# A streaming-encoder block in float32: the operand's first transposes moved ahead of the gain vector's, and the weight groups of the first FFN begun after 16 standard steps in place of 12

## The chip, the cores and the metric

One core of one Trainium2 chip. The metric is the device time of one execution in microseconds; lower is better. Three timed runs of the kernel before are shown, and one execution was profiled.

## What is computed

One block over 256 frames of width 2048, in float32:

```python
x = x + 0.5 * swiglu_ffn(rmsnorm(x, g1), w_gate, w_up, w_down)      # D_FF = 5632
h = rmsnorm(x, gm)
proj = h @ w_in                                                     # 2048 x 11264
x = x + (sigmoid(gate_a) * attention(...) @ w_out_att
         + sigmoid(gate_r) * retention(...) @ w_out_ret) @ w_out
x = x + 0.5 * swiglu_ffn(rmsnorm(x, g2), w_gate2, w_up2, w_down2)
out = rmsnorm(x, gf)

def swiglu_ffn(x, w_gate, w_up, w_down):
    return (silu(x @ w_gate) * (x @ w_up)) @ w_down
```

The change touches the opening of the program and the first of the two FFNs.

## The kernel before

**Tiles.** The frames are two tiles of 128 (t = 0, 1). The transposed activations are the stationary operand of TensorE, the weights are streamed past it in tiles of 256 rows by 512 columns (0.5 MB). Float32 is kept by splitting both sides in a high and a low part: `split` (line 126, 127) casts a weight tile to its high part on ScalarE (`hi`) and subtracts on VectorE what is left (`lo`); `three` (lines 137, 138, 140) then makes three matmuls of 512 columns for each product: high by high, high by low, low by high. The split buffers are four (`SPLIT_BUFS`), the buffers of unsplit tiles five (`RAW_BUFS`).

**Steps.** The program is one list of steps, written in order. A *standard* step takes one weight tile for both frame tiles: 12 matmuls, one split. A *group* (class `Strassen`) makes the up and gate product of one block of 512 columns together, in 28 steps of 6 matmuls: three phases of eight steps (tiles `z12...`: group, phase, number, `r` or `s`) and a fourth of four. In the first phase VectorE also adds a pair of tiles for four of the steps (line 528), in the second it adds (line 583) and subtracts (line 570), and POOL then issues a transfer that accumulates into the tile (line 571). So a group step of the first two phases costs VectorE up to two operations of full size, where a standard step costs it one. The groups' unsplit tiles (`z12k`, `z12x`) are loaded by POOL (line 539), all others by SP (line 117).

**The order.** `weave` (line 670 on) first puts `lead` standard steps in the list. Then, behind each pair of a group's steps, it adds a standard step whenever its credit allows, unless the next standard job needs blocks that are not there yet (`needs`, `at_hand`). The standard jobs of the FFN are the gate and up products of blocks 9 and 10, eight steps each, and the down products in seven passes. The first is gate 9, then up 9, gate 10, and the down product of blocks 9 and 0:

```python
for _ in range(lead):
    next_standard()
rate = (len(queue) - apart) / (len(groups) * sum(SHARE))
```

The tiles of the first group are asked for eight steps ahead of it (`first = len(steps) - 8`), and POOL issues them behind a tiny operation that waits for the third block of the operand (`third_block`, line 804).

**The norm's work.** `Norm.put` (line 449) transposes two blocks of x on TensorE, scales them by the gain on ScalarE (line 462) and splits them (446, 447). It is called in the opening and in steps 1 to 6. The sums of blocks that the groups use as operands (`s5`, `s6`, `s3`, `s7`) are made by `add_up` on VectorE (lines 483 to 497, tiles `n1f`, `n1s5l` ...), up to step 18. The squares are summed on ScalarE in steps 8 to 11, and POOL raises the result to the power -0.5 (`n1rstd`, line 373). The gate of block 9 is passed through Silu in step 12; line 742 is the eviction of its up product (`f1g`), line 377 the low part of its transposes (`f1a9l`).

**The opening.** SP loads x and the first weight tiles; ACT's queue loads the identity and the gain vector. `turn` transposes the gain vector on TensorE (line 292) and copies it on VectorE (293). Then `prep_upto(1)` splits the first weight tile, here with casts on VectorE (line 161), and `n1.put(0, 0)` transposes the first two blocks.

Of the kernel before, what the change touches and what calls it, by code (L numbers as in the profile page):

```python
# [27 lines left out]
KC = 2  # L28
# [7 lines left out]
TAIL = 4  # L36
AHEAD = (2, 3)
HALF_K = D // P // 2
LEAD = 12
MIX_LEAD = 8  # L40
RET_WAIT = (14, 5)
HELD = 6
# [3 lines left out]
PASSES = ((9, 0), (1, 2), (10, 3), (4, 5), (6,), (7,), (8,))  # L46
# [26 lines left out]
def block_kernel(ctx: ExitStack, tc: tile.TileContext, x, g1, w1g, w1u, w1d, gm, w_in, rel, woa, wor, wo,  # L73
# [32 lines left out]
    def later(n, fn):  # L106
        due.setdefault(state["step"] + n, []).append(fn)
# [124 lines left out]
    def prep_upto(n):  # L232

        while state["prep"] < min(len(steps), n) and state["slots"]:
            s = steps[state["prep"]]
            load_some()
            state["slots"] -= 1
            s.prep()
            for ring in s.frees:
                room[ring] += 1  # L240
            state["prep"] += 1
        load_some()
# [142 lines left out]
    class Operand:  # L385
# [11 lines left out]
        def put(self, b, t, src):  # L397

            hi, lo = self.alloc(b)
            ts = slice(t * P, (t + 1) * P)  # L400
            ps = transpose4(src, f"{self.name}p{b}{t}").rearrange("p (i q) -> p i q", i=4)
            split_out(ps, hi[:, :, ts], lo[:, :, ts])
# [5 lines left out]
    class Norm:  # L408
# [37 lines left out]
            nc.scalar.copy(hi[:, js, :], src)  # L446
            nc.vector.tensor_sub(lo[:, js, :], src, hi[:, js, :].bitcast(F32))

        def put(self, b, half):
            if half == 0:  # L450
                self.raw[b] = act_tile(F32, f"{self.name}x{b}")
            raw = self.raw[b]
            ps = side_tile(f"{self.name}p{b}{half}")
            for i in range(2):
                k = 4 * b + 2 * half + i
                for t in range(NT):
                    nc.tensor.transpose(
                        ps[:, (2 * i + t) * P : (2 * i + t + 1) * P], xs[t][:, k * P : (k + 1) * P], id_sb
                    )
            for i in range(2):  # L460
                k = 4 * b + 2 * half + i
                nc.scalar.activation(
                    raw[:, 2 * half + i, :], ps[:, i * SEQ : (i + 1) * SEQ], AF.Copy, scale=self.gain[:, k : k + 1]
                )
            j = 4 * (b // 2) + 2 * half
            for t in range(NT):
                src = raw[:, 2 * half : 2 * half + 2, t * P : (t + 1) * P]
                self.split_to(f"a{t}{b % 2}", slice(j, j + 2), src)
            if half == 1 and not self.sums:
                del self.raw[b]  # L470
            elif half == 1 and b % 2 == 1:
                for i, key in enumerate(self.SUMS):
                    later(1 + 3 * i, lambda key=key: self.add_up(b // 2, key))
# [238 lines left out]
    def ffn(name, norm, wg, wu, wd, after, start=None):  # L712


        nblocks = DFF // NB
        mids, ready = {}, {}

        def put_mid(b, hs):
            mids[b] = Operand(f"{name}a{b}", 1)
            for t in range(NT):  # L720
                mids[b].put(0, t, hs[t])

        def plain(b):
            gates = {}

            wait = GATE_WAIT if start is not None and b == PLAIN[0] else 0

            def gate_done(acc):
                def go():
                    for t in range(NT):  # L730
                        gates[t] = tmp_tile(f"{name}g{b}{t}", "gate", 2)
                        nc.scalar.activation(gates[t], acc[t], AF.Silu, scale=norm.scale(t))

                if wait:
                    later(wait, go)
                else:
                    go()

            def up_done(acc):
                for t in range(NT):  # L740
                    a = gates[t]
                    nc.vector.scalar_tensor_tensor(a, acc[t], norm.scale(t), a, op0=ALU.mult, op1=ALU.mult)  # L742
                later(4, lambda: put_mid(b, gates))

            tags = ("acc", "acc")
            up = Gemm(wu, 0, b * NB, D // P, norm, up_done, tags)
            up.makes = b
            return [Gemm(wg, 0, b * NB, D // P, norm, gate_done, ("z", "z") if wait else tags), up]

        def paired(b):  # L750
            got = {}

            def evict(t, side, r):
                if side == 1:
                    nc.scalar.activation(r, r, AF.Silu)
                    got[t] = r
                    return
                nc.vector.scalar_tensor_tensor(got[t], r, norm.scale(t), got[t], op0=ALU.mult, op1=ALU.mult)
                if t == 1:
                    later(4, lambda: put_mid(b, got))  # L760

            return Strassen(norm, wu, b * NB, wg, b * NB, evict)

        def down(blocks, last):

            jobs = []

            def act(k, t):
                return mids[blocks[k // 4]](k % 4, t)

            for b in range(D // NB):
                cols = slice(b * NB, (b + 1) * NB)

                def seed(acc, t, cols=cols):
                    nc.scalar.activation(acc, xs[t][:, cols], AF.Copy, scale=2.0)  # L775

                def evict(acc, t, cols=cols):
                    nc.scalar.activation(xs[t][:, cols], acc, AF.Copy, scale=0.5)  # L778

                if last:  # L780
                    job = Gemm(wd, 0, b * NB, 4 * len(blocks), act, down_done(b, 0.5, after))
                else:
                    job = Gemm(wd, 0, b * NB, 4 * len(blocks), act, None, ("acc", "acc"), seed)
                    job.evict = evict
                job.rows = [(m * 4 + i) * P for m in blocks for i in range(4)]
                job.needs = blocks
                jobs.append(job)
            return jobs

        downs = {blocks: down(blocks, blocks is PASSES[-1]) for blocks in PASSES}  # L790
        first, second = [plain(b) for b in PLAIN]
        order = [first, second[:1], downs[PASSES[0]], second[1:]] + [downs[p] for p in PASSES[1:]]
        jobs = [job for part in order for job in part]
        for job, follow in zip(jobs, jobs[1:]):
            job.next = follow
        groups = {b: (lambda b=b: paired(b)) for b in range(nblocks) if b not in PLAIN}
        weave(jobs, len(downs[PASSES[-1]]) * len(PASSES[-1]) * 4 // KC + HELD, groups, LEAD, start)


    n1 = Norm("n1", gains[:, 0, :], True)  # L800
# [221 lines left out]
    def gates(col1, col2, func, dsts):  # L1022
# [13 lines left out]
    groups = {  # L1036
        b: (lambda b=b: gates(GA + b * NB, GG + b * NB, AF.Sigmoid, merge_dram[b])) for b in range(D // NB)
    }
# [97 lines left out]
    turn = load_gain(g1, 0, nc.scalar)  # L1136
# [25 lines left out]
    load_one()  # L1162
    load_x(2 * NB, 3 * NB)
    load_x(3 * NB, 4 * NB)
    turn()
    prep_upto(1)
    n1.put(0, 0)
    for fn in first_low:
        fn()
    n1.put(0, 1)  # L1170
# [87 lines left out]
```

## Time and profile before

| | us |
|---|---|
| median of 3 runs | 2061.78 |
| the runs | 2060.89 to 2064.99 |
| the profiled execution, its own time | 2063.49 |
| its span, first to last instruction | 2061.4 |
| TensorE busy | 2045.3 (99%) |
| VectorE busy | 1754.4 (85%) |
| ScalarE busy | 1402.9 (68%) |

The busy shares are averages over the whole span. A stretch in which VectorE is busy all the time and TensorE is not stands out only when the span is cut in windows.

### The profile page before, as it was taken

How to read it: one execution, taken by the hardware profiler on the slowest of the kernel's cores; microseconds unless marked ns; L12 is line 12 of the kernel's file. 1: busy time of each engine (PE TensorE's matmuls, PEld its weight loads, DVE VectorE, ACT ScalarE, POOL GpSimd, SP SyncE). 2: the span in 40 equal slices, each digit the busy share in tenths (PEclk: the TensorE clock that was granted, in tenths of full speed). 3: DMA queues.
4: the chain of work that ended last, by engine and by line, in shares of the span. 5: the costliest groups of instructions: out<-in, count | busy, mean ns of one | idle time of the engine just before them, and what ended most of it. 6: DMA issues, size and time to landing. Idle time of an engine off the chain costs nothing.

```text
span 2061.4 us, 26148 instructions
## 1 busy us (share of the span) xinstructions
PE 2045.3 (99%) x9256; PEld 1691.9 (82%) x9256; DVE 1754.4 (85%) x1824; ACT 1402.9 (68%) x1732; POOL 273.3 (13%) x322
## 2 busy tenths in 40 slices
PE   9999999999999999999999999999999999999998
PEld 7788888888888888888888888888888878888886
DVE  7998899899997799899966667568989988998986
ACT  7677667777777767776665434556776677677785
POOL 1111211122111110122100000010122012110200
PEclk9999999999999999999999999999999999999999
DMA  8776876788678777788775645575787668876873
GB/s 308 207 225 230 269 227 207 239 264 258 191 231 258 240 205 251 258 284 260 227 267 175 223 143 187 187 245 170 235 273 234 200 224 273 240 206 233 281 215 133
DMA packets 219315, 473.28 MB, mean 230 GB/s; under 512 B 14816, under 2 KB 15568, under 8 KB 219184
## 3 DMA queue, kind: packets, MB, share of 16 engines
q1 hardware_dynamic: 161088, 309.89, 44.7%
q0 software_dynamic: 54752, 155.88, 27.9%
q10 hardware_dynamic: 3344, 5.84, 0.8%
q8 instruction: 72, 1.18, 0.2%
q14 instruction: 59, 0.48, 0.1%
HBM read 462.65 MB, written 8.91 MB: 229 GB/s over the span
## 4 chain that ended last, share of the span: by engine, by line
PE 93%; DVE 3%; DMA 2%; ACT 1%; issue 1%; SPq 0%; DVEq 0%; POOLq 0%; POOL 0%; ACTq 0%
PE acc L140 17%; PE acc L137 17%; PE acc L138 17%; DMA raw<-in_ffn_w_down_dram 2%; DVE lo L127 1%; ACT hi L126 0%; PE z684a L140 0%; PE z380a L137 0%; PE z953a L138 0%; PE z684a L138 0%; PE z418a L137 0%; PE z723a L138 0%; PE z380a L140 0%; PE z281a L138 0%; PE z723a L137 0%
## 5 line engine op out<-in xcount | busy, mean ns | idle before, releaser
L127 DVE TENSOR_TENSOR lo<-raw,hi 128x1024 fp32r<-128x1024 f32 x399 | 487.1, 1224 | 179.1 <-ACT hi L126 174.3
L126 ACT CAST hi<-raw 128x1024 fp32r<-128x1024 f32 x399 | 417.7, 1050 | 226.8 <-PE acc L138 143.7
L775 ACT ACTIVATE acc<-xall 128x512 f32<-128x512 f32 x96 | 57.5, 599 | 8.0 <-DVE f1g L742 3.6
L778 ACT ACTIVATE xall<-acc 128x512 f32<-128x512 f32 x96 | 56.6, 589 | 9.2 <-PE acc L140 7.4
L137 PE MATMUL acc<-hi,mgh 128*128 128x512 f32 x128 | 50.2, 392 | 0.0
L138 PE MATMUL acc<-hi,mgl 128*128 128x512 f32 x128 | 49.9, 390 | 0.0
L137 PE MATMUL acc<-hi,nma01h 128*128 128x512 f32 x96 | 38.7, 403 | 0.0
L137 PE MATMUL acc<-hi,nma00h 128*128 128x512 f32 x96 | 38.6, 402 | 0.0
L138 PE MATMUL acc<-hi,nma00l 128*128 128x512 f32 x96 | 37.5, 391 | 0.0
L137 PE MATMUL acc<-hi,nma10h 128*128 128x512 f32 x96 | 37.5, 391 | 0.0
L138 PE MATMUL acc<-hi,nma01l 128*128 128x512 f32 x96 | 37.5, 390 | 0.0
L138 PE MATMUL acc<-hi,nma11l 128*128 128x512 f32 x96 | 37.5, 390 | 0.0
L137 PE MATMUL acc<-hi,nma11h 128*128 128x512 f32 x96 | 37.4, 390 | 0.0
L138 PE MATMUL acc<-hi,nma10l 128*128 128x512 f32 x96 | 37.4, 390 | 0.0
L140 PE MATMUL acc<-lo,mgh 128*128 128x512 f32 x128 | 35.6, 390 | 0.0
L140 PE MATMUL acc<-lo,nma01h 128*128 128x512 f32 x96 | 29.6, 390 | 0.0
L140 PE MATMUL acc<-lo,nma00h 128*128 128x512 f32 x96 | 29.6, 390 | 0.0
L140 PE MATMUL acc<-lo,nma11h 128*128 128x512 f32 x96 | 29.6, 390 | 0.0
L140 PE MATMUL acc<-lo,nma10h 128*128 128x512 f32 x96 | 29.6, 390 | 0.0
L140 PEld LDWEIGHTS acc<-lo,mgh 128*128 128x128 f32 x128 | 24.0, 188 | 5.0
L137 PEld LDWEIGHTS acc<-hi,mgh 128*128 128x128 f32 x128 | 24.1, 188 | 4.9
L138 PEld LDWEIGHTS acc<-hi,mgl 128*128 128x128 f32 x128 | 24.1, 188 | 4.8
(6130 smaller groups left out, 6933.7 us busy)
## 6 DMA issues: line engine op xcount, KB each, us to landing
raw<-in_ffn_w_down_dram SPq DMA_DIRECT2D x176, 512.0 KB, 6.1
raw<-in_w_in_dram SPq DMA_DIRECT2D x96, 512.0 KB, 4.7
raw<-in_ffn_w_up_dram SPq DMA_DIRECT2D x32, 512.0 KB, 10.2
raw<-in_w_out_dram SPq DMA_DIRECT2D x32, 512.0 KB, 4.0
raw<-in_ffn_w_gate_dram SPq DMA_DIRECT2D x31, 512.0 KB, 5.9
raw<-in_w_out_att_dram SPq DMA_DIRECT2D x16, 512.0 KB, 4.3
raw<-in_w_out_ret_dram SPq DMA_DIRECT2D x16, 512.0 KB, 4.0
z380x<-in_w_in_dram POOLq DMA_DIRECT2D x8, 512.0 KB, 7.4
```

The source lines that it names most:

```text
L126: nc.scalar.copy(hi, raw)
L127: nc.vector.tensor_sub(lo, raw, hi.bitcast(F32))
L137: nc.tensor.matmul(acc, ahi, whi, start=first, stop=False, **more)
L138: nc.tensor.matmul(acc, alo, whi, start=False, stop=False, **more)
L140: nc.tensor.matmul(acc, ahi, wlo, start=False, stop=last, **more)
L775: nc.scalar.activation(acc, xs[t][:, cols], AF.Copy, scale=2.0)
L778: nc.scalar.activation(xs[t][:, cols], acc, AF.Copy, scale=0.5)
```

## The change

Two edits. In the opening, `put` takes a function and calls it between its transposes and its scaling; the call passes the gain's transpose and the first split, so four transposes of x come first. In `weave`'s call the lead becomes a pair: 16 for the first FFN (the only call with a `start`), 12 for the second as before.

```diff
-LEAD = 12
+LEAD = (16, 12)
...
-        def put(self, b, half):
+        def put(self, b, half, meanwhile=None):
...
                     nc.tensor.transpose(
                         ps[:, (2 * i + t) * P : (2 * i + t + 1) * P], xs[t][:, k * P : (k + 1) * P], id_sb
                     )
+            if meanwhile is not None:
+                meanwhile()
             for i in range(2):
...
-        weave(jobs, ..., groups, LEAD, start)
+        weave(jobs, ..., groups, LEAD[start is None], start)
...
-    turn()
-    prep_upto(1)
-    n1.put(0, 0)
+
+    n1.put(0, 0, lambda: [turn(), prep_upto(1)])
```

**The opening on TensorE.** `pswz` and `pswacc` are warming matmuls, `gps` is the gain vector's transpose, `n1p` the operand's. Before:

```order
L1145 MATMUL pswz_118<-warm 128x512
L292 MATMUL gps_138<-id_sb,grows_109 128x16
L457 MATMUL n1p_150<-id_sb,xall 128x128 x4
L457 MATMUL n1p_167<-id_sb,xall 128x128 x4
L1145 MATMUL pswacc_113<-warm 128x512
```

Now (lines below the edits count two more):

```order
L1147 MATMUL pswz_118<-warm 128x512
L457 MATMUL n1p_139<-id_sb,xall 128x128 x4
L292 MATMUL gps_144<-id_sb,grows_109 128x16
L457 MATMUL n1p_167<-id_sb,xall 128x128 x4
L1147 MATMUL pswacc_113<-warm 128x512
```

The gain vector's transpose stands behind four of the operand's transposes; all else keeps its place.

**VectorE in the second phase of group 0.** Tiles `lo_...` are standard splits, `loz121...` (before) and `loz161...` (now) those of the group's second phase. Before:

```order
L127 TENSOR_TENSOR loz1210s<-z12x_338,hiz1210s 128x1024
L570 TENSOR_TENSOR z12k_306<-z12x_338,z12k_306 128x1024
L742 SCALAR_TENSOR_TENSOR f1g_553<-acc_0_448,n1rstd,f1g_553 128x512
L742 SCALAR_TENSOR_TENSOR f1g_555<-acc_1_449,n1rstd,f1g_555 128x512
L127 TENSOR_TENSOR loz1212r<-rawz1212r,hiz1212r 128x1024
L583 TENSOR_TENSOR z12x_462<-z12x_462,rawz1212r 128x1024
L127 TENSOR_TENSOR lo_744<-raw_626,hi_743 128x1024
L127 TENSOR_TENSOR loz1211s<-z12x_411,hiz1211s 128x1024
L570 TENSOR_TENSOR z12k_371<-z12x_411,z12k_371 128x1024
L127 TENSOR_TENSOR loz1213r<-rawz1213r,hiz1213r 128x1024
L583 TENSOR_TENSOR z12x_514<-z12x_514,rawz1213r 128x1024
L377 TENSOR_TENSOR f1a9l_775<-f1a9p_776,f1a9h_774 128x4x128
```

Now:

```order
L127 TENSOR_TENSOR loz1610s<-z16x_454,hiz1610s 128x1024
L572 TENSOR_TENSOR z16k_426<-z16x_454,z16k_426 128x1024
L127 TENSOR_TENSOR loz1612r<-rawz1612r,hiz1612r 128x1024
L585 TENSOR_TENSOR z16x_568<-z16x_568,rawz1612r 128x1024
L127 TENSOR_TENSOR lo_828<-raw_746,hi_827 128x1024
L127 TENSOR_TENSOR loz1611s<-z16x_508,hiz1611s 128x1024
L572 TENSOR_TENSOR z16k_482<-z16x_508,z16k_482 128x1024
L127 TENSOR_TENSOR loz1613r<-rawz1613r,hiz1613r 128x1024
L585 TENSOR_TENSOR z16x_610<-z16x_610,rawz1613r 128x1024
L127 TENSOR_TENSOR lo_871<-raw_774,hi_870 128x1024
L127 TENSOR_TENSOR loz1612s<-z16x_568,hiz1612s 128x1024
L572 TENSOR_TENSOR z16k_540<-z16x_568,z16k_540 128x1024
```

The evictions of block 9 (`f1g`) and its low parts (`f1a9l`) have left this place; they stand in the first phase, behind the first two steps of the group. Of the operations on the norm's forms, 11 stood between the group's first split and the end of its second phase, and now five. The standard splits in these two phases are seven in both orders.

**VectorE from the end of group 0 into group 1.** `loz123...` and `loz163...` are group 0's fourth phase, `loz510...` and `loz520...` group 1's first. Before:

```order
L127 TENSOR_TENSOR loz1223s<-z12k_489,hiz1223s 128x1024
L127 TENSOR_TENSOR lo_1001<-raw_874,hi_1000 128x1024
L127 TENSOR_TENSOR loz1230s<-z12x_338,hiz1230s 128x1024
L127 TENSOR_TENSOR loz1231s<-z12x_411,hiz1231s 128x1024
L758 SCALAR_TENSOR_TENSOR z12c_882<-z12b,n1rstd,z12c_882 128x512
L127 TENSOR_TENSOR loz1232s<-z12x_462,hiz1232s 128x1024
L127 TENSOR_TENSOR loz1233s<-z12x_514,hiz1233s 128x1024
L643 TENSOR_TENSOR z12c_1037<-z12c_1037,z12s_708 128x512
L127 TENSOR_TENSOR lo_1071<-raw_888,hi_1070 128x1024
L127 TENSOR_TENSOR loz5100r<-z51k_906,hiz5100r 128x1024
L528 TENSOR_TENSOR z51x_950<-z51x_950,z51k_906 128x1024
L127 TENSOR_TENSOR loz5101r<-z51k_974,hiz5101r 128x1024
```

Now:

```order
L127 TENSOR_TENSOR loz1623s<-z16k_589,hiz1623s 128x1024
L127 TENSOR_TENSOR loz1630s<-z16x_454,hiz1630s 128x1024
L127 TENSOR_TENSOR loz1631s<-z16x_508,hiz1631s 128x1024
L127 TENSOR_TENSOR loz1632s<-z16x_568,hiz1632s 128x1024
L760 SCALAR_TENSOR_TENSOR z16c_954<-z16b,n1rstd,z16c_954 128x512
L127 TENSOR_TENSOR loz1633s<-z16x_610,hiz1633s 128x1024
L127 TENSOR_TENSOR loz5200r<-z52k_978,hiz5200r 128x1024
L530 TENSOR_TENSOR z52x_1004<-z52x_1004,z52k_978 128x1024
L645 TENSOR_TENSOR z16c_1099<-z16c_1099,z16s_782 128x512
L127 TENSOR_TENSOR loz5201r<-z52k_1042,hiz5201r 128x1024
L530 TENSOR_TENSOR z52x_1054<-z52x_1054,z52k_1042 128x1024
L127 TENSOR_TENSOR loz5200s<-z52x_1004,hiz5200s 128x1024
```

The two standard splits (`lo_1001`, `lo_1071`) are gone from here. In the new order the last standard split of group 0 stands ten group splits ahead of group 1, and the next (`lo_1219`) behind the eighth of group 1: 18 group splits in a row. Group 0 holds eight standard steps (11 before), group 1 twelve (10), the later ones ten each (10 or 11).

On POOL the same change of numbers puts `n1rstd` behind four of group 0's eight loads; before, it stood behind all eight. On SP three tiles of gate 10 stand ahead of the first tile of the group's second phase. The counts of instructions and transfers are the same on every engine.

## Rows read from the trace of the kernel before

**Rows 1.** The page: the chain that ended last, by engine.

```profile
PE 93%; DVE 3%; DMA 2%; ACT 1%; issue 1%; SPq 0%; DVEq 0%; POOLq 0%; POOL 0%; ACTq 0%
```

**Rows 2.** Waits of PE, 30 to 700 us: total us, times, longest us.

```profile
PE f1a9p L382 <- DVE f1g L742: 1.0, 1, 1.0
PE acc L140 <- DVE lo L127: 0.7, 2, 0.5
```

**Rows 3.** Windows: us; busy PE, PEld, DVE, ACT, POOL; PEclk, DMA share, GB/s.

```profile
70.00:88.00 18.00, 16.39 (x73) 12.19 (x71) 18.00 (x19) 9.97 (x12) 4.30 (x4) 1.00 0.83 208
88.00:106.00 18.00, 18.00 (x81) 14.91 (x80) 15.04 (x14) 11.17 (x13) 7.86 (x11) 1.00 1.04 329
106.00:128.00 22.00, 22.00 (x103) 18.32 (x102) 21.38 (x22) 16.92 (x21) 0.00 (x0) 1.00 0.59 210
```

**Rows 4.** Timeline of PE, 66 to 90 us: start us, us, engine, line, operation.

```profile
67.59 0.39 PE L137 MATMUL z12c<-hiz1211r,n1s3h 128*128 128x512 f32 x1
...
68.95 0.39 PE L137 MATMUL z12a<-hiz1210s,n1s6h 128*128 128x512 f32 x1
...
71.43 1.31 PE L382 MATMUL f1a9p<-id_sb,f1g 128*128 128x128 f32 x8 [0.96 <-DVE f1g L742]
72.50 0.48 PE L137 MATMUL z12c<-hiz1212r,n1s3h 128*128 128x512 f32 x1
...
86.33 0.40 PE L137 MATMUL acc<-hi,n1a01h 128*128 128x512 f32 x1
```

**Rows 5.** Timeline of PE, 0 to 45 us.

```profile
5.21 0.20 PE L292 MATMUL gps<-id_sb,grows 16*128 16x16 f32 x1 [0.96 <-DMA grows<-in_norm_ffn_g_dram]
...
8.27 0.51 PE L138 MATMUL acc<-hi,n1a00l 128*128 128x512 f32 x1 [0.41 <-DVE n1a00l L447]
```

**Rows 6.** Timeline of DVE, 0 to 45 us.

```profile
5.45 0.18 DVE L293 COPY gains<-gps 128x16 f32<-128x16 f32 x1 [5.45 <-PE gps L292]
...
7.46 0.43 DVE L161 CAST hi<-raw 128x512 fp32r<-128x512 f32 x1 [0.83 <-DMA raw<-in_ffn_w_gate_dram]
7.80 0.42 DVE L447 TENSOR_TENSOR n1a00l<-n1x,n1a00h 128x256 fp32r<-128x256 f32 x1
...
39.42 0.68 DVE L489 SCALAR_TENSOR_TENSOR n1f<-n1f,n1x 128x512 f32<-128x512 f32 x1
40.02 0.69 DVE L497 TENSOR_TENSOR n1s5l<-n1f,n1s5h 128x512 fp32r<-128x512 f32 x1
```

**Rows 7.** Timeline of DVE, 66 to 90 us.

```profile
70.63 1.41 DVE L742 SCALAR_TENSOR_TENSOR f1g<-acc,n1rstd,f1g 128x512 f32<-128x512 f32 x2
71.95 1.22 DVE L127 TENSOR_TENSOR loz1212r<-rawz1212r,hiz1212r 128x1024 fp32r<-128x1024 f32 x1
73.08 1.22 DVE L583 TENSOR_TENSOR z12x<-z12x,rawz1212r 128x1024 f32<-128x1024 f32 x1
...
79.89 1.28 DVE L377 TENSOR_TENSOR f1a9l<-f1a9p,f1a9h 128x512 fp32r<-128x512 f32 x2
81.09 1.22 DVE L127 TENSOR_TENSOR lo<-raw,hi 128x1024 fp32r<-128x1024 f32 x1
```

**Rows 8.** Timeline of DVE, 86 to 130 us.

```profile
108.54 1.23 DVE L127 TENSOR_TENSOR loz1233s<-z12x,hiz1233s 128x1024 fp32r<-128x1024 f32 x1
109.69 0.68 DVE L643 TENSOR_TENSOR z12c<-z12c,z12s 128x512 f32<-128x512 f32 x1
110.36 1.23 DVE L127 TENSOR_TENSOR lo<-raw,hi 128x1024 fp32r<-128x1024 f32 x1
```

**Rows 9.** Timeline of PE, 108 to 130 us.

```profile
113.15 0.61 PE L140 MATMUL z12a<-loz1233s,n1a11h 128*128 128x512 f32 x2
```

**Rows 10.** Timeline of POOL, 0 to 80 us.

```profile
20.61 0.91 POOL L539 DMA_DIRECT2D z12k<-in_ffn_w_up_dram  x1
...
45.08 0.72 POOL L373 TENSOR_TENSOR n1rstd<-v,mhalf 128x2 f32<-128x2 f32 x1 [18.49 <-DVE v L372]
```

**Rows 11.** DMA issues, 86 to 116 us: xcount, KB each, median us to landing.

```profile
z51x<-in_ffn_w_gate_dram POOLq DMA_DIRECT2D x4, 512.0 KB, 11.8
```

More of the change, by code (lines that the diff above doesn't have):

```diff
@@ L796, in ffn @@
         groups = {b: (lambda b=b: paired(b)) for b in range(nblocks) if b not in PLAIN}
-        weave(jobs, len(downs[PASSES[-1]]) * len(PASSES[-1]) * 4 // KC + HELD, groups, LEAD, start)
+        weave(jobs, len(downs[PASSES[-1]]) * len(PASSES[-1]) * 4 // KC + HELD, groups, LEAD[start is None], start)
     n1 = Norm("n1", gains[:, 0, :], True)
```

## The prediction

> **What bounds the kernel now.** I read the page first, then who TensorE waited for, then the timelines of the two places that the change touches. The chain that ended last runs 93% on TensorE [rows 1]. So the change can only give back time in which TensorE stands, or make it stand anew. In the first FFN after the opening the table of waits is led by two lines, both behind VectorE, together 1.7 us [rows 2]. One stretch holds nearly all of it, the second phase of group 0: VectorE is busy 18.00 of 18.00 us there and TensorE 16.39 [rows 3].
>
> How much that stretch loses I take from steps, not from idle time. A step of a group is six matmuls and starts 1.36 us after the one before it (67.59 to 68.95) [rows 4]; a standard step is twelve, 2.72. From 68.95 to 86.33 TensorE did six group steps (8.16), two standard ones (5.44) and the eight transposes of block 9, which took 1.07 (71.43 to 72.50) [rows 4]: 14.67 us of work in 17.38. **The loss is 2.7 us.** The Trainium skill (Perfetto Trace Analysis, Identifying the Most-Contended Engine) says that matmul busy time is a bad measure of TensorE because matmuls are pipelined. The rows agree: the idle shown in that stretch is 18.00 less 16.39, 1.6 us, and going by it the gain below would be 1.1 us smaller.
>
> **Part 1, the first transposes ahead of the gain vector's.** In the profile the gain transpose waits 0.96 us for its DMA and starts at 5.21, and the operand's transposes follow it [rows 5]. In the changed order four of them can start when x and the identity are there, at the latest when the vector landed, so TensorE's part may move forward by up to 0.3 us. What follows? The first ACT scaling needs the gains as well as the transposes; the gains are copied from 5.45 to 5.63 [rows 6], and behind the four transposes (about 0.11 us each) that copy comes no earlier. ScalarE may start its scaling 0.1 us sooner. But the second matmul, at 8.27, waited for the low part of the operand [rows 5], and VectorE makes that at 7.80, right behind a cast that waited 0.83 us for the second half of the first weight tile and began at 7.46 [rows 6]. That tile's transfer, the SP queue and VectorE's order are untouched. So the later start costs and gives **nothing**; what covers the gained 0.1 to 0.3 us is the landing of the weights. No DMA is added or moved on SP or ACT here. Bounds: 0 to 0.4 us of gain (the wait of 0.41 before 8.27), taken as 0 because the row names the releaser.
>
> **Part 2, what is removed: group 0 gets out of the norm's way.** Sixteen standard steps now precede group 0 instead of twelve. Counts of steps, matmuls and DMAs are the same; only places change. I compare VectorE's work with TensorE's over the group's first two phases. A full-size VectorE operation follows the next by 1.13 us (71.95 to 73.08), the evictions of block 9 took 1.32 (70.63 to 71.95), its low parts 1.20 (79.89 to 81.09) [rows 7]; a half-size operation on the norm's forms takes 0.60 (39.42 to 40.02) [rows 6].
>
> Before: 16 splits and 12 sums (28 x 1.13 = 31.6), seven standard splits (7.9), block 9's 1.3 and 1.2, and 11 half-size operations (6.6): 48.6 us. TensorE: 16 x 1.36 + 7 x 2.72 + 1.07 = 41.9. VectorE is short by 6.7 us, and 2.7 were lost, so its lead (up to four split buffers ahead) covered 4.0. After: only five of the half-size operations are left inside (3.0), seven standard splits as before: 45.0 against 41.9, short by 3.1. That is under 4.0, so **the 2.7 us go**.
>
> **What is added: a run without standard steps.** Eight standard steps now stand in group 0 where eleven stood, because block 10's gate has only eight and the next job, the down product, may not begin before block 0 is there. The order shows 18 group splits in a row, the last ten of group 0 and the first eight of group 1. Through the third and fourth phase VectorE holds, with one operation of 1.13 per step of 1.36. Then the first two phases of group 1 come: 28 x 1.13 = 31.6, four standard splits (4.5), the evictions of block 0 (110.36 less 109.69, 0.67 each, two: 1.3) [rows 8] and its low parts (1.2): 38.6. TensorE: 16 x 1.36 + 4 x 2.72 + 1.07 = 33.7. Short by 4.9. The lead on entry: the last split of group 0 ended at 109.77 [rows 8] and was used at 113.15 [rows 9], 3.4 us. So 1.5 us would be lost; the very last sum (1.13) is waited for by no split, so 0.4 at the least. I take the middle, **1.0 us**, and round up to 1.1 for the transposes, which wait for the late evictions. Bounds: 0 (a lead of over 4.9), and 4.9 (no lead on entry, which is how group 0 of before ended its second phase, VectorE at 18.00 of 18.00 [rows 3]). After this stretch standard steps follow every pair again and VectorE recovers; the remaining groups have ten each, against ten or eleven, which lost nothing between 88 and 128 us [rows 3].
>
> **The queues.** On SP three weight tiles of the gate move ahead of the group's; no issue is added. On POOL the vector rstd's power, which ran at 45.08, now stands behind four of the group's eight loads, which went out from 20.61 [rows 10], and the other four wait behind it. They leave at about 45.8 to 48; with 11.8 us to landing in the busiest stretch [rows 11] the last is there at 60. It is added at about 66, when group 0, begun 10.9 us later (four standard steps), reaches its fourth pair: 6 us of cover. In ScalarE's order squares, table load and Silu keep their step numbers. All cost nothing.
>
> **Sum.** 0 - 2.7 + 1.1 = -1.6 us. The profiled execution took 2063.49, 1.7 above the median of 2061.78; from the median the result is **2060.2 us**. A measurement of this kernel tells about 0.2% (4.1 us) from no change, so I forecast no change.
>
> **The rivals.**
> - *The lead covers the run of group steps.* Nothing is lost again: 2061.8 - 2.7 = 2059.1. For it: the 0.4 us of the lower working. Against it: the lead cannot grow while the split buffers are four.
> - *The opening counts.* If the first matmuls were bound by ScalarE's scaling, 0.4 us more come: 2059.8. Against it: the row that names the weight tile [rows 6].
> - *VectorE enters group 1 with no lead.* All 4.9 us are lost: 2061.8 - 2.7 + 4.9 = 2064.0, a change that doesn't do what its second half says. For it: VectorE ran without any gap for 18 us in group 0 [rows 3]. Against it: one operation a step in the two phases ahead gives it 0.2 us a step to recover.
> - *Late tiles (the other side).* Group 1's eight tiles of 0.52 MB are issued behind the accumulating transfers of group 0, and four standard steps (10.9 us) fewer now lie between their place in the order and the group's fourth sum. By my count of steps they begin at about 92 us and are needed by about 124. In between 8.9 MB must land: two accumulations, read and written, 2.1; the eight tiles, 4.2; five tiles of SP's, 2.6. At 329 GB/s, the rate of 88 to 106 [rows 3], that takes 27 us and ends at 119, in time. It decides from 278 GB/s down (8.9 MB in 32 us); at the 210 GB/s of 106 to 128 [rows 3] it is 42 us, ten late: 2061.8 - 1.6 + 10 = 2070.2, slower by 0.4%. Against it: in that row the rate was low because the queues had little left to move.
>
> **How the numbers follow.** Forecast 55%; covered run 20%; opening 7%; no lead 13%; late tiles 5%. The single runs shown spread from 2060.89 to 2064.99, so each case carries about 1 us to either side. From 2059.1 less 0.7 to just short of 2064.0 leaves out the late tiles and half of the case with no lead: 2058.4 to 2063.7. Faster by over 0.2% would be under 2057.7, below every case: 3%. Slower by over 0.2% is above 2065.9, the late tiles alone: 5%. No change: 92%.
>
> **What would show it.** In the changed profile the operand's first four transposes should start before the gain vector's, and the second matmul at 8.2 to 8.3 as now. Group 0's second phase should show no wait on VectorE, and block 9's transposes no wait of 1 us. New waits on VectorE of 0.2 to 0.5 us each should stand in group 1's first two phases, some 120 to 145 us in. The forecast is wrong if those waits are longer than the 2.7 us removed, if they name a DMA, if the first matmuls start by 0.3 us or more earlier, or if waits come up in later groups.

## The result and the profile after

| | before | after |
|---|---|---|
| median | 2062.88 | 2068.76 |
| lowest to highest | 2060.89 to 2065.55 | 2067.38 to 2071.66 |
| runs | 8 | 8 |

The ratio is 1.0028 [1.0017, 1.0039]: **slower by 5.9 us**. The forecast was 2060.2 and its range ended at 2063.7. The profiled execution took 2071.66 us, its span is 2069.5. It is the slowest of the eight and 8.2 us above the profiled execution of before, so part of that difference lies outside the stretch looked at below.

The chain that ended last (the page of the changed kernel) still runs on TensorE nearly all the time; against [rows 1] two points have gone from PE to DVE and DMA:

```profile
PE 91%; DVE 4%; DMA 3%; ACT 1%; issue 1%; SPq 0%; DVEq 0%; POOLq 0%; POOL 0%; ACTq 0%
```

The waits of PE from 30 to 700 us, the view of [rows 2] (total us, times, longest us):

```profile
PE acc L140 <- DVE lo L127: 3.3, 6, 0.6
PE acc L137 <- ACT hi L126: 0.8, 1, 0.8
PE z16a L137 <- ACT z16c L642: 0.8, 1, 0.8
PE z52c L140 <- DVE loz5202s L127: 0.2, 1, 0.2
```

The line for block 9's transposes (`f1a9p`) is gone, as forecast. In its place stand six waits of about half a microsecond on VectorE, one on a weight cast and one on `z16c`, an eviction of group 0's own bank. The second phase of group 0, whose window in the kernel before is the first of [rows 3] (us; busy PE, PEld, DVE, ACT, POOL; PEclk, DMA share, GB/s), is now:

```profile
81.00:99.00 18.00, 18.00 (x81) 14.92 (x80) 18.00 (x17) 10.88 (x12) 7.71 (x8) 1.00 0.97 245
```

VectorE is as full as it was, and TensorE has no gap: an engine that is busy all the time need not be late.

**Loss by group.** A wait in this view is smaller than what it costs, so I add up loss as in the prediction, by starts: for each matmul the time to the next one's start, beyond the spacing of an undisturbed stretch (1.36 us for six, [rows 4]: 0.227; 0.109 for a transpose). The table gives these sums in us, from one profiled execution each; a group's stretch begins with its first matmul, that of group 8 includes the down products behind it. An undisturbed group shows 0.10 to 0.14, so the method has little noise of its own. From one execution to another of like kernels a group can differ by up to 0.9 (group 8 of e1_open_alone and of before, which have the same order there), and the opening ranges from 4.9 to 6.3 over kernels with one and the same opening. The medians and ratios are of the timed runs; each ratio is against runs of before made alongside, whose medians were 2062.9 to 2063.4.

| | open | G0 | G1 | G2 | G3 | G4 | G5 | G6 | G7 | G8+ | sum | median | ratio to before |
|---|---|---|---|---|---|---|---|---|---|---|---|---|---|
| before | 5.5 | 3.1 | 0.1 | 0.1 | 1.1 | 0.1 | 0.1 | 0.1 | 0.1 | 3.0 | 13.4 | 2062.88 | |
| after | 5.6 | 1.2 | 4.3 | 0.1 | 1.8 | 1.0 | 0.1 | 1.0 | 0.1 | 3.6 | 18.9 | 2068.76 | 1.0028 |
| e1_open_alone | 5.2 | 3.1 | 0.2 | 0.6 | 1.0 | 0.1 | 0.1 | 0.1 | 0.1 | 2.1 | 12.6 | 2062.71 | 0.9998 [0.9990, 1.0007] |
| e2_lead_alone | 6.2 | 1.2 | 4.0 | 0.2 | 2.4 | 1.2 | 0.2 | 1.0 | 0.1 | 3.4 | 20.0 | 2068.81 | 1.0029 [1.0018, 1.0040] |
| e3_shift | 5.3 | 1.2 | 4.2 | 0.1 | 3.8 | 0.1 | 1.1 | 0.1 | 0.1 | 4.1 | 20.2 | 2067.90 | 1.0024 [1.0015, 1.0032] |
| e4_up_ahead | 5.1 | 0.1 | 0.4 | 1.2 | 0.1 | 1.0 | 0.1 | 1.0 | 0.1 | 3.7 | 12.8 | 2062.52 | 0.9996 [0.9987, 1.0005] |
| e5_lead13 | 5.7 | 2.2 | 0.1 | 0.1 | 1.4 | 0.1 | 2.0 | 0.2 | 0.6 | 4.0 | 16.4 | 2065.71 | 1.0009 [1.0000, 1.0018] |
| e6_rate | 5.6 | 3.0 | 0.1 | 1.0 | 0.4 | 1.0 | 0.1 | 1.0 | 0.1 | 7.9 | 20.1 | 2070.29 | 1.0034 [1.0021, 1.0046] |
| e7_up_ahead_15 | 5.9 | 0.1 | 0.2 | 0.1 | 0.1 | 0.1 | 0.1 | 0.1 | 0.1 | 3.0 | 9.8 | 2059.13 | 0.9978 [0.9969, 0.9987] |
| e8_hold_turn | 6.1 | 0.1 | 8.1 | 0.1 | 1.8 | 1.0 | 0.1 | 1.1 | 0.1 | 4.0 | 22.6 | 2069.98 | 1.0035 [1.0023, 1.0047] |
| e9_hold_three | 4.9 | 1.1 | 0.8 | 0.1 | 2.5 | 2.0 | 0.1 | 1.5 | 0.1 | 3.4 | 16.5 | 2065.15 | 1.0008 [1.0000, 1.0017] |
| e10_up_ahead_shift | 6.3 | 0.1 | 0.6 | 0.1 | 0.1 | 0.5 | 0.1 | 1.2 | 1.3 | 2.4 | 12.8 | 2060.34 | 0.9985 [0.9976, 0.9994] |

After loses 5.5 us more than before in this stretch, and the medians differ by 5.9. Group 0 gained 1.9; groups 1, 3, 4, 6 and 8 lost 7.3. The rows show three places. First TensorE's timeline (start us, us, engine, line, operation, idle before it and what ended it):

```profile
4.64 0.76 PE L457 MATMUL n1p<-id_sb,xall 128*128 128x128 f32 x4 [0.39 <-DMA xall<-in_x_dram]
5.33 0.23 PE L292 MATMUL gps<-id_sb,grows 16*128 16x16 f32 x1
...
8.00 0.50 PE L138 MATMUL acc<-hi,n1a00l 128*128 128x512 f32 x1 [0.37 <-DVE n1a00l L447]
...
110.40 0.61 PE L140 MATMUL z16a<-loz1623s,n1s7h 128*128 128x512 f32 x2
111.79 0.50 PE L137 MATMUL z16a<-hiz1630s,n1a11h 128*128 128x512 f32 x1 [0.78 <-ACT z16c L642]
...
131.62 0.73 PE L140 MATMUL acc<-lo,f1a9h 128*128 128x512 f32 x2 [0.48 <-DVE lo L127]
...
170.89 0.50 PE L137 MATMUL acc<-hi,f1a0h 128*128 128x512 f32 x1 [0.85 <-ACT hi L126]
...
332.36 0.74 PE L140 MATMUL acc<-lo,f1a1h 128*128 128x512 f32 x2 [0.57 <-DVE lo L127]
```

*The turn of group 0.* I call the place between a group's third and fourth phase its turn. The fourth phase (`hiz1630s`) accumulates onto the bank `z16a` that the third has just filled, and ScalarE must copy that bank first (L642). Before, a standard step stood there (`lo_1001` in the order shown ahead; the steps of [rows 8, 9] follow it); now the gate has run out, and TensorE stands: 111.79 less 110.40, less two matmuls of 0.227, is 0.94, and the next matmul is 0.1 late: 1.05 us.

*Group 1.* Its windows (us; busy PE, PEld, DVE, ACT, POOL; PEclk, DMA share, GB/s):

```profile
116.00:122.00 6.00, 6.00 (x28) 4.98 (x27) 6.00 (x7) 4.42 (x5) 0.00 (x0) 1.00 0.63 227
122.00:130.00 8.00, 7.69 (x38) 5.75 (x36) 7.94 (x9) 4.12 (x6) 0.00 (x0) 1.00 0.00 1
130.00:140.00 10.00, 9.52 (x42) 7.57 (x42) 10.00 (x10) 7.94 (x9) 0.00 (x0) 1.00 0.56 170
...
168.00:176.00 8.00, 7.08 (x31) 5.20 (x30) 5.47 (x5) 6.17 (x9) 1.45 (x2) 1.00 1.05 386
```

VectorE is busy throughout while TensorE is not, the picture that [rows 3] showed for group 0 of before. From 122 to 130 the transfer engines moved 1 GB/s. SP had no free buffer: from 90 to 180 us it waited for standard splits on VectorE (total us, times, longest us), first in the kernel before, then in this one:

```profile
SPq L117 <- DVE lo L127: 41.2, 14, 9.8
SPq L117 <- DVE lo L127: 50.2, 12, 24.8
```

From 168 to 176 the engines are full, and a weight tile is late. Of the 4.3 us, 2.6 lie behind VectorE and 1.5 behind that tile. That the idle stretch made the tile late is argued; e9_hold_three below agrees with it, but changes more than this.

*Groups 4, 6 and 8.* Each loses 0.8 to 0.9 us at its first standard step (332.36, and the like at 465.69 and 599.01), where before lost nothing. Why it is late shows ScalarE's timeline at the turn of group 3, with the late cast at 170 us above it, for the tile of group 1:

```profile
169.79 1.04 ACT L126 CAST hi<-raw 128x1024 fp32r<-128x1024 f32 x1 [2.21 <-DMA raw<-in_ffn_w_down_dram]
...
321.57 0.60 ACT L777 ACTIVATE acc<-xall 128x512 f32<-128x512 f32 x1
322.10 0.58 ACT L780 ACTIVATE xall<-acc 128x512 f32<-128x512 f32 x1
322.71 0.60 ACT L777 ACTIVATE acc<-xall 128x512 f32<-128x512 f32 x1
323.25 0.58 ACT L780 ACTIVATE xall<-acc 128x512 f32<-128x512 f32 x1
323.73 1.04 ACT L126 CAST hiz13033s<-z130x 128x1024 fp32r<-128x1024 f32 x1
```

and VectorE's behind it:

```profile
324.80 1.23 DVE L127 TENSOR_TENSOR loz13033s<-z130x,hiz13033s 128x1024 fp32r<-128x1024 f32 x1 [1.85 <-ACT hiz13033s L126]
...
331.08 1.22 DVE L127 TENSOR_TENSOR lo<-raw,hi 128x1024 fp32r<-128x1024 f32 x1
```

A down product of 512 columns ended exactly at the turn. Its results are evicted to x and the next ones seeded from x: four ScalarE operations, 2.2 us, stand ahead of the group's last cast. VectorE stands 1.85 us just before the stretch that needs its lead, and the first standard split of group 4 begins at 331.08, 3.1 us after the group (328.0).

### The profile page after: what moved, and what is told of

Same layout as the page of the kernel before. It is cut to its first block, busy times and chain, and to the rows that moved or that the text cites. A ratio compares the mean times of both kernels' runs of the same rounds, so it can differ in the third digit from the quotient of the medians.

```text
span 2069.5 us, 26147 instructions
## 1 busy us (share of the span) xinstructions
PE 2049.4 (99%) x9256; PEld 1690.2 (82%) x9256; DVE 1754.6 (85%) x1824; ACT 1401.7 (68%) x1732; POOL 273.3 (13%) x322
## 4 chain that ended last, share of the span: by engine, by line
PE 91%; DVE 4%; DMA 3%; ACT 1%; issue 1%; SPq 0%; DVEq 0%; POOLq 0%; POOL 0%; ACTq 0%
PE acc L140 17%; PE acc L137 16%; PE acc L138 16%; DMA raw<-in_ffn_w_down_dram 2%; DVE lo L127 1%; DMA raw<-in_w_in_dram 1%; ACT hi L126 0%; PE z684a L140 0%; PE z380a L140 0%; PE z723a L137 0%; PE z282a L137 0%; PE z953a L137 0%; PE z838a L137 0%; PE z723a L138 0%; PE z418a L137 0%
```

## The experiments

Three theories, each with its rival. **T1:** behind group 0 there is a stretch without standard steps, in which VectorE cannot keep up; that is group 1's loss. **T2:** a standard job that ends at a turn costs the next group about 0.9 us; with a lead of 16 the credit rate is exactly ten steps to a group, and the ends of the down products (four steps each) fall on the turns of groups 3, 5 and 7. **The opening** is nothing. The rivals: the tiles come too late or too early with the new lead, or the rate itself costs.

**e1_open_alone** and **e2_lead_alone**, the two halves:

```diff
-LEAD = (16, 12)
+LEAD = (12, 12)
```
```diff
-    n1.put(0, 0, lambda: [turn(), prep_upto(1)])
+    turn()
+    prep_upto(1)
+    n1.put(0, 0)
```

> The opening edit alone, lead 12 in both FFNs. Theory of the steps (the loss comes from where the standard steps stand, the opening is worth what the second matmul's start shows, 8.27 before and 8.00 in the changed kernel): 0.3 us under before, no change that can be told, and losses in the groups as before (group 0 loses 3.1 us). Rival (the opening edit delays something later): near the changed kernel, 5.9 us over before.

> The lead of 16 alone, opening as before. Theory of the steps: as the changed kernel plus 0.3 us, so 6 us over before, with 4 us lost in group 1 and 0.9 us at the start of groups 4, 6 and 8. Rival (the opening): as before. Rival (the two edits only hurt together): between, under 3 us over before.

Measured: 0.9998 [0.9990, 1.0007] and 1.0029 [1.0018, 1.0040]. The opening alone is no change, and the lead alone is the whole loss, group by group as in after.

**e3_shift**, one step of credit taken at group 3, so that jobs no longer end at the turns:

```diff
+            if start is not None and n == 3:
+                credit -= 1
```

> The changed kernel with one standard step of group 3 put off (the credit starts one lower there), so that every later standard step stands one place further on and no down job ends at a turn (the place between a group's third and fourth phase). Theory that down jobs ending at the turn cause the later losses: groups 4, 6 and 8 lose 0.1 to 0.3 us each in place of about 1, so 2.6 us under the changed kernel, 2066; group 1 still loses 4. Rival (ten standard steps a group are too few wherever they stand): as the changed kernel, the losses of 1 us remain or move to other groups.

Measured: 2067.90, about 0.9 below after, where more was expected; the two intervals do not tell it from after. Groups 4 and 6 fell from 1.0 to 0.1, as T2 has it. But the edit has a price, in PE's waits from 30 to 700 us:

```profile
PE acc L137 <- ACT hi L126: 2.5, 4, 1.1
PE acc L140 <- DVE lo L127: 1.5, 3, 0.6
PE z130c L140 <- DVE loz13013r L127: 1.1, 1, 1.1
```

Group 3 lost a standard step of its first phases and stands on VectorE (`loz13013r`); of the four waits on casts after had one, three more came up in groups 3, 5 and 8. A partial miss: right for the two groups named, not for the time.

**e4_up_ahead**, the run of group splits taken away by a job that needs nothing: block 10's up product stands ahead of the first down product.

```diff
+        if start is not None:
+            order = [first, second] + [downs[p] for p in PASSES]
```

> The changed kernel with the up product of block 10 put right behind its gate product, ahead of the first down product, so that standard steps are there all through groups 0 and 1 and the run of 18 group splits is gone. Theory of the run: group 0 loses 0.1 in place of 1.2 us and group 1 at most 0.3 in place of 4.2; down jobs now end at the turns of groups 1, 3, 5 and 7, so one more loss of 0.9 in group 2: 2068.8 - 5.0 + 0.9 = 2064.7. Rival (late tiles: transfers of group 1 queue behind those of group 0): the transfers are the same or more in that stretch, group 1 still loses 3 us or more, over 2067.

Measured: 2062.52, better than the 2064.7 expected. Groups 0 and 1 lose 0.1 and 0.4: T1 is right, and the lead of 16 as such costs nothing there. Group 3 fell from 1.8 to 0.1, which no theory had in it. In this order jobs end at the turns of groups 1, 3, 5 and 7, and groups 2, 4, 6 and 8 lose 1.2, 1.0, 1.0 and about 0.8: T2 at new places.

**e5_lead13** and **e6_rate** go back to the kernel before and change the rate (e5 the lead too, to 13), without and with job ends at the turn:

```diff
-LEAD = 12
+LEAD = (13, 12)
...
+        if start is not None:
+            rate = (len(queue) + -3 - apart) / (len(groups) * sum(SHARE))
```
```diff
+        if start is not None:
+            rate = (len(queue) + -4 - apart) / (len(groups) * sum(SHARE))
```

> The kernel before with the lead of the first FFN 13 in place of 12, and the credit rate that belongs to a lead of 16 (ten standard steps in every group). The order of the jobs and the opening are those of before. In this order no standard job ends at a turn (between a group's third and fourth phase), and no more than eight group splits follow each other. Theory T1 + T2 (a run of group splits and job ends at the turn are what the change lost): only group 0 loses, some 2.5 us to the norm's operations, and groups 1 to 8 lose 0.1 each as undisturbed groups do: about 2061.5, the kernel before 2063. Rival R (a lead above 12, or the rate of 1.0 in itself, costs: the tiles of the later groups come too early or too late): groups 4, 6 and 8 lose 0.9 or more again as in the changed kernel, 2064 to 2066.

> As e5_lead13 in everything but the lead: 12, as in the kernel before. With it jobs end at the turns of groups 1, 3, 5 and 7, with no standard step behind the fourth phase; there is no long run of group splits. T2: the groups behind them, 2, 4, 6 and 8, lose 0.9 to 1.2 us each, so it is 3.5 to 4 us above e5_lead13, about 2065.3, with no change at all in the lead against before. Rival (job ends at the turn are harmless, and only the lead of 16 or the run of group splits behind group 0 makes the later losses): as before, 2062 to 2063.5, and groups 2, 4, 6, 8 lose 0.1 each.

e6 is the cleanest case of T2. TensorE's timeline, the first standard step of groups 2, 4, 6 and 8:

```profile
184.26 0.74 PE L140 MATMUL acc<-lo,f1a9h 128*128 128x512 f32 x2 [0.54 <-DVE lo L127]
...
318.56 0.73 PE L140 MATMUL acc<-lo,f1a1h 128*128 128x512 f32 x2 [0.57 <-DVE lo L127]
...
451.78 0.73 PE L140 MATMUL acc<-lo,f1a10h 128*128 128x512 f32 x2 [0.57 <-DVE lo L127]
...
584.99 0.73 PE L140 MATMUL acc<-lo,f1a4h 128*128 128x512 f32 x2 [0.57 <-DVE lo L127]
```

Four waits, one in every second group, each 0.8 us by starts, and nothing in the groups between but group 3's 0.4. So T2 holds without the lead of 16 and without any run of splits.

It is not true of every such end, though. In the kernel before a down product ends at the turn of group 4 as well, and VectorE stands there too:

```profile
382.26 1.23 DVE L127 TENSOR_TENSOR loz16633s<-z166x,hiz16633s 128x1024 fp32r<-128x1024 f32 x1 [1.39 <-ACT hiz16633s L126]
...
384.00 1.22 DVE L127 TENSOR_TENSOR lo<-raw,hi 128x1024 fp32r<-128x1024 f32 x1
```

Yet group 5 loses 0.1. Two things differ there: a standard step stands behind the fourth phase (its split is the one at 384.00), and group 5's first standard step comes behind its second pair, not its first. Which of the two saves it was not tried.

The whole of e6 is slower than expected, 2070.3: another 5 us go at the end of group 8, which T2 had not in it.

```profile
662.64 0.66 PE L382 MATMUL f1a8p<-id_sb,z316c 128*128 128x128 f32 x4 [3.02 <-DVE gains L293]
```

The next norm's gain vector is transposed there at a fixed step, and in this order it came between the two halves of block 8's transposes; they waited 3.0 us for VectorE's copy, and then TensorE's clock was down (below). That is a collision of its own.

e5 missed: 2065.7, where 2061.5 was expected. Groups 2, 4 and 6 are at 0.1 and 0.2, so the place that T2 speaks of is quiet. But groups 3, 5, 7 and 8 lose 1.4, 2.0, 0.6 and about 1, mostly within their third phases. ScalarE's timeline:

```profile
435.51 1.05 ACT L126 CAST hiz20323r<-rawz20323r 128x1024 fp32r<-128x1024 f32 x1 [1.88 <-DMA rawz20323r<-in_ffn_w_up_dram]
...
439.57 1.04 ACT L126 CAST hiz20323s<-z203k 128x1024 fp32r<-128x1024 f32 x1
```

The tile came 1.9 us late with the transfer engines full (387 GB/s from 432 to 437), and a job that ended in the middle of the third phase put its four operations (437.42 to 439.57) ahead of the group's next cast. The late tile is not special: the same one of each group was waited for by ScalarE for 0.8 to 3.3 us in some groups of all kernels looked at so, before and e7_up_ahead_15 included, mostly at no loss. What made it cost here, and not in e7_up_ahead_15, where jobs end at the same place of groups 2, 4, 6 and 8 at 0.1 us, I could not settle.

**e7_up_ahead_15**, no run of splits and no job end at a turn (ten steps in each group, at most six group splits in a row):

```diff
-LEAD = (16, 12)
+LEAD = (15, 12)
...
+        if start is not None:
+            rate = (len(queue) + -1 - apart) / (len(groups) * sum(SHARE))
...
+        if start is not None:
+            order = [first, second] + [downs[p] for p in PASSES]
```

> The changed kernel with three edits in the first FFN: the up product of block 10 stands ahead of the first down product (as in e4_up_ahead), the lead is 15, and the rate stays that of 16. Every group then has ten standard steps, no run of group splits is longer than six, and no job ends at a turn. T1 + T2: the opening and group 0 as in e4_up_ahead (5.1 and at most 0.6), all other groups about 0.1, the last 2.9: the first FFN loses 9.5 us against 13.4 in the kernel before, so about 2059 to 2059.5, which is below both kernels. Rival R (losses of this kind go with the groups' tiles or with VectorE's load, not with where jobs end): losses of 1 us stay in three or four groups as in e4_up_ahead, about 2062.5.

Measured: 2059.13, ratio 0.9978 [0.9969, 0.9987], as T1 and T2 had it, and **faster than both kernels**. All that PE waited for from 30 to 700 us:

```profile
PE nmp L457 <- DVE xall L656: 0.5, 2, 0.3
PE z319a L137 <- ACT hiz31923s L126: 0.2, 1, 0.2
```

The seam of groups 3 and 4 beside that of after: no eviction ahead of the last cast, no gap on VectorE, and the first standard split 1.7 us after the group's start (318.7) in place of 3.1:

```profile
314.12 1.22 DVE L127 TENSOR_TENSOR loz12933s<-z129x,hiz12933s 128x1024 fp32r<-128x1024 f32 x1
...
320.40 1.22 DVE L127 TENSOR_TENSOR lo<-raw,hi 128x1024 fp32r<-128x1024 f32 x1
```

**e8_hold_turn** and **e9_hold_three** ask what of T1 is the run's length and what its place. After, with gate steps of group 0 held back: one for the turn, then three (one for the turn, two for group 1's first phase).

```diff
+                if start is not None and n == 0 and i in (8, 9, 10):
+                    continue
```
```diff
+                if start is not None and n == 0 and i in (5, 7, 8, 9, 10, 12, 13, 14, 15):
+                    continue
```

> The changed kernel, but group 0 holds its last step of block 10's gate back for the turn, where its fourth phase accumulates onto the bank that the third has filled and ScalarE copies first. The counts are the same; the step moves from the middle of the third phase to its end. Theory: the wait of about 1.05 us at the turn goes (a standard step of 2.72 us covers the copy); the run of group splits shrinks from 18 to 12, so VectorE has a shorter way to its next one: group 1 loses 1.5 to 3 us where it lost 4.2. About 2066 to 2067.5. Rival (the wait at the turn and the losses of group 1 are one delay, which comes out wherever the run stands): no difference, 2068.5 to 2069.

> The changed kernel, but group 0 holds three of block 10's eight gate steps back: one for the turn, two for the first phase of group 1 (behind its first and second pair; the first phase of group 1 then has four standard steps as in the kernel before it had three, where it has one in the changed kernel). The run of group splits moves into the third phase of group 0 (nine in a row), where VectorE has one operation a step. T1a (what costs is a first phase of a group with one standard step, VectorE having twelve operations for the eight steps, not the length of the run): the wait at the turn (1.05) goes, and so do the 2.2 us of waits on VectorE in group 1, and with them the idle transfer engines at 122 to 130 us and the late tile behind them (1.25): groups 0 and 1 together lose 0.5 to 1.5 us where the changed kernel lost 5.4; groups 4, 6 and 8 still lose 0.9 each, as jobs still end at the turns of groups 3, 5 and 7: 2064 to 2065.5. T1b (a run costs wherever it stands, since TensorE needs splits faster than VectorE delivers them): group 0 now loses 2 to 4 us in its third and fourth phase, 2067 to 2069.

e8: the wait at the turn is gone (group 0 at 0.1), so that term is shown. But group 1 went from 4.3 to 8.1, though the run was shortened from 18 to 12: behind VectorE it lost 3.9 where after lost 2.6, and the late tile in group 1 grew:

```profile
172.60 0.50 PE L137 MATMUL acc<-hi,f1a0h 128*128 128x512 f32 x1 [1.84 <-ACT hi L126]
```

The edit made a case of T2 of its own. The step it holds back is the last of block 10's gate, so this job now ends at the turn of group 0. ScalarE's operations at that end (110.33 to 112.63, the gate's Silu among them) stand ahead of the group's last cast, and VectorE stands just before group 1:

```profile
110.86 1.35 ACT L736 ACTIVATE f1g<-acc,n1rstd 128x512 f32<-128x512 f32 x2
...
112.63 1.04 ACT L126 CAST hiz1633s<-z16x 128x1024 fp32r<-128x1024 f32 x1
...
113.70 1.23 DVE L127 TENSOR_TENSOR loz1633s<-z16x,hiz1633s 128x1024 fp32r<-128x1024 f32 x1 [2.01 <-ACT hiz1633s L126]
```

VectorE began the first split of group 1 at 115.45, 1.4 us ahead of TensorE; in after it was 3.3 us ahead (114.11 and 117.37). So e8 does not tell what the run's length is worth. In sum 1.0035 [1.0023, 1.0047], no gain; my expectation of 2066 to 2067.5 failed, and 2069.98 is above its rival's 2069 too. e9: group 1 falls from 4.3 to 0.8 and the whole to 2065.15, inside the expectation of T1a, below that of T1b; groups 0 and 1 together lose 1.9, a little more than T1a had, and groups 3, 4 and 6 lose more than in after, group 8 about the same. Its window of the stretch in which after moved 1 GB/s:

```profile
122.00:130.00 8.00, 8.00 (x37) 6.63 (x36) 7.76 (x9) 6.60 (x9) 0.00 (x0) 1.00 0.35 103
```

TensorE has no gap, tiles come in, and the stand near 170 us is 0.2 us only. The run of group splits into group 0's third phase (ten by VectorE's order, nine by the expectation) cost 0.9 near its start (a wait of 0.6 on `loz1620r`, 92.79): T1b's mechanism, below its price of 2 to 4 us. So a run of ten there is cheap. The runs point to the place: a group's *first* phase, with twelve VectorE operations to eight steps, needs its standard steps among them. That length counts for nothing is not shown, since no kernel changed the length alone.

**e10_up_ahead_shift**, e4_up_ahead with the credit one less at group 1:

```diff
+            if start is not None and n == 1:
+                credit -= 1
```

> e4_up_ahead with one edit: the credit is one less at group 1, so that from there on every standard step stands one place later, and no job ends at a turn (in e4_up_ahead those of groups 1, 3, 5 and 7 did). The price: the first phase of group 1 has two standard steps where it had three. T2: the losses of groups 2, 4, 6 and 8 (1.21, 0.99, 0.96 and some 0.8) go, group 1 loses up to 1 us more: 3 us less than e4_up_ahead, 2059.5 to 2060.5. Rival (what made e7_up_ahead_15 faster than e4_up_ahead is its lead of 15, not the place where jobs end): as e4_up_ahead, 2062 to 2063.

Measured: 2060.34, as T2 had it and not its rival: same lead as e4_up_ahead, a median 2.2 us less (the two intervals just overlap), group 2 from 1.2 to 0.1 and group 4 from 1.0 to 0.5. The sums of the two profiles are equal, 12.8, since the opening of this execution was 1.2 slower and groups 6 and 7 lost more. Its one wait of PE from 30 to 700 us, 0.7 us, is behind a cast in the third phase of group 7, and group 6 loses 0.7 in the same place: the loss that e5_lead13 showed and that stays open.

## Why the prediction was wrong

- **Part 1, the opening: right in its sum.** Alone the edit measures 0.9998. In after the second matmul came at 8.00 in place of 8.27 [rows 5]; it still waits for the low part behind the cast of the second half of the weight tile, as the step said, and that half landed earlier in this execution. That 0.27 is no gain of the edit: in the eight profiles with the new opening the second matmul came between 7.79 (e9_hold_three) and 9.52 (e10_up_ahead_shift). Two readings of the step were off. The first transposes moved by 0.70 (4.64 in place of 5.34), not 0.3 at most: x had landed by then. And the weight tile does not always cover: in e7_up_ahead_15 x landed late, the gain's copy behind its transposes came at 6.75, the casts waited for no weights, and the second matmul came at 9.48.
- **Part 2, removed, 2.7 us: right.** Group 0 loses 0.1 with its turn covered (e4_up_ahead, e8_hold_turn) where it lost 3.1. In after itself 1.2 stay, because of the next point. The sign it went by is weaker than it looked: VectorE is at 18.00 of 18.00 in after's second phase too, at no loss.
- **A term that was missing: the turn, 1.05 us.** The prediction saw that the gate runs out in group 0 and counted VectorE's splits, but not that a standard step is forced at the turn to cover ScalarE's copy of the bank. e8_hold_turn shows it.
- **"The run without standard steps", 1.1 us: measured 4.1.** The mechanism is right and its size wrong, by 3 us, the largest miss of the sum; two of its steps failed. First, it set the work of group 1's two phases against each other as a whole, four standard steps included; but three of those come behind the first phase and cannot help it. From `loz5200r` at 114.11 VectorE needs until 131.57 for the eight splits, four sums, block 0's operations and the first standard split; TensorE, from 117.37, wants that split after 8 x 1.36 + 1.07 + 4 x 0.227 = 12.9 us, at 130.2. That alone is over 1 us, and the later standard splits lose again: 2.6 behind VectorE. Second, no term stood for what the run does to the transfers: 8 us with no buffer to load into, then a tile whose wait cost 1.5 (that the one made the other is argued, see above).
- **"The remaining groups have ten each, which lost nothing": the step whose mechanism failed.** It took one stretch without waits as a sample for all groups. Their number of steps is not what counts but where jobs end, and what stands between such an end and the next group. Groups 4, 6 and 8 cost 0.9, 0.9 and 0.6 more than before; e6_rate (there without the lead), e3_shift and e10_up_ahead_shift (gone or smaller with a shift) show the cause. Group 3's 0.7 more is not chance: it is one wait of 0.63 for a standard split at 295.90, in the second phase, and e2, e3, e8 and e9 have the same wait (0.61 or 0.62) where before and e1 have none above 0.1. VectorE has no gap from 275.12 to the split it waits for, at 294.62, and block 10's low parts stand in there (282.07). In e4, e7 and e10, where block 10 is finished earlier, group 3 loses 0.1. No run changed this alone, so its cause is argued.
- **Sum by the runs:** -3.0 + 1.05 + 4.1 + 2.4 + 0.7 = 5.3, and 5.5 by the table, against 5.9 by the medians.
- **The rivals.** *No lead* came nearest in what it charged group 1 (4.9; 4.1 were measured), but not by its condition: VectorE entered group 1 about 3 us ahead (`loz1633s` ended at 113.93, and its matmul started at 116.91), close to the 3.4 counted on. *Late tiles* was right that a tile would be late, but in a standard step at 170 us, for 1.5 us in place of ten. *The lead covers the run* and *the opening counts* were wrong. "Waits come up in later groups" stood among the signs of error, but no case with a chance held it.

The Trainium skill (Perfetto Trace Analysis, Identifying the Most-Contended Engine) says that matmul busy time is not a good measure of how close TensorE is to its limit. Rows agree again: 0.57 idle at 332.36 cost 0.84 by starts, since the matmul before the wait starts 0.96 ahead of the next one, and that one 0.34, where 0.227 is undisturbed.

## What to carry to other kernels

When a list of steps is shifted against another, look up where every job's *last* step lands and what filler stands behind it, because its evictions queue on an engine that feeds the next stretch; a rate that comes out as a whole number repeats one bad landing again and again. A filler step helps only the work behind it, so a shortfall is summed from the start of a stretch to each single use, not over the stretch. And a step that looks like filler may be the cover of a bank's copy: ask of each what waits behind it.

## What the runs showed of the hardware

**After a stand of 1.84 us the clock was halved for a time; after one of 0.85 it was not.** In e8_hold_turn, windows of TensorE's granted clock (column PEclk) behind the wait that ended at 172.60:

```profile
168.00:172.00 4.00, 2.76 (x13) 1.95 (x11) 0.87 (x1) 0.49 (x1) 0.00 (x0) 1.00 1.03 383
...
175.00:176.00 1.00, 1.00 (x4) 0.81 (x3) 1.00 (x2) 1.00 (x2) 0.72 (x1) 0.50 1.04 373
```

That is 1.2 GHz in place of 2.4; eight matmuls from 174.8 on start 0.427 apart, 1.6 us lost behind the wait. After has the same wait at 170.89 with 0.85 and stays at 1.00 (168 to 176, above). In e6_rate the clock fell likewise behind the stand of 3.0.

**Two queues share the transfer engines by packets, not by bytes.** In after, from 105 to 119 us, with the engines full (q0 is POOL's queue, q1 SP's; packets, MB, share):

```profile
q0 software_dynamic: 965, 3.50, 65.7%
q1 hardware_dynamic: 968, 1.88, 37.3%
```

Equal packets, but POOL's are 3.6 KB and SP's 1.9, so in this stretch the groups' tiles on POOL's queue come nearly twice as fast as the tiles on SP's, those of the standard steps among them. The Trainium skill (DMA: Bandwidth & Descriptors, Queues, rings and completion order) says that an engine takes turns between queues packet by packet; the counts agree. Whether smaller packets on POOL's queue would bring the late tiles in time wasn't tried.
